# A macaron block of two SwiGLU layers around a pool and RWKV-7 mixer: the first modulation block summed on TensorE, the stored tiles multiplied from the first two rows of tiles on, and the modulation tiles of the first layer sent for three ahead

## The chip, the cores and the metric

The kernel runs on one core of a Trainium2 chip, in f32. A time is the device time of one execution in microseconds. Before the change three runs took 2119.42, 2113.76 and 2109.96 us, a median of 2113.76. One more execution was profiled and took 2117.75 us.

The engines are called as the profile calls them: PE is TensorE's matmul, PEld its weight load, DVE is VectorE, ACT is ScalarE, SP is SyncE, which here only sends DMAs.

## What is computed

A residual stream x of 256 tokens by 2048 passes three sublayers: a SwiGLU layer, a mixer, and a second SwiGLU layer. Each is normalised, modulated and gated by nine vectors of 2048 that come from one product of a conditioning vector with a wide matrix.

```python
mod = (jax.nn.silu(c) @ w_ada[l] + b_ada[l]).reshape(B, N_SUBLAYERS, N_MOD, D_MODEL)
...
h = modulate(rms_norm(x, gain_pre), shift, scale)      # h * (1 + scale) + shift
y = rms_norm(fn(h), gain_post)
return x + weight * (1 + gate[:, None, :]) * y
...
def swiglu(h, w_gate, w_up, w_down):
    return (jax.nn.silu(h @ w_gate) * (h @ w_up)) @ w_down
```

Here w_ada is 2048 by 18432 (151 MB), w_gate and w_up are 2048 by 5632, and w_down is 5632 by 2048. Every weight is read once. Only the first layer's beginning is touched by the change.

## The kernel before

**Precision.** PE multiplies in a fast f32 form, so each operand is split: hi is the operand rounded to that form, lo what is left. For the weights ACT writes hi (line 185) and DVE writes lo = raw - hi (line 186). The normalised input hT has both halves too. One weight product of the reference becomes three on PE: hi with both halves of hT, lo with the first.

**Tiles.** The model dimension is 16 rows of tiles (k = 0 to 15), each 128 long. In the first stage of a SwiGLU layer 20 of the 44 column tiles of w_gate and w_up are taken, in 10 loads of four tiles each. The first two loads (four columns of gate and four of up) keep their sums in four PSUM banks over all 16 rows. The other eight loads belong to the stored tiles (FF_SPILL = 16): each has two free banks for a block of rows, and what the block gives is copied by ACT (line 669) into SBUF, or added to it by DVE (line 671) in later blocks. The method outer runs this: for each block of rows it first makes hT for the block, then goes through the 10 loads.

**Blocks.** FIRST_BLOCKS cuts the rows into (0, 2), (2, 2), (4, 4), (8, 4), (12, 4): start and count. With MERGE = 4 the stored tiles leave out the first block and take rows 0 to 3 at once in the second. So the first block has two loads with 24 weight products each, and PE has nothing else until the second block's hT is there.

**Modulation.** hT of a block needs the shift and the scale vector for the block's rows (vectors 0 and 1). Their columns of w_ada come in DMAs (line 247, tiles called ada, 4 buffers of 512 KB; a block of two rows has eight such tiles), each tile holds two of the 16 contraction rows for both vectors, and DVE multiplies each by its column of silu(c) and adds it to acc (lines 255 and 257). Then PE sums acc over the partitions by a product with a vector of ones (line 201, mm<-ones,acc), DVE adds the bias (line 326, mod) and makes the gain (line 413, gs), PE transposes and normalises x by a product with a diagonal scale (mm<-scale,x), and ACT writes hT from that (line 425), and a copy (line 429, work) from which DVE makes the second half of hT (line 430).

**What sets the order.** A scheduler puts the instructions of each engine in one order when the kernel is built; each engine then works its queue strictly in that order, and so does SP. Buffers are rings: four raw, four ada, four hi and lo, eight PSUM banks. In the first layer ada_step sends for a part of the modulation and sums it at once. It is called at loads 1, 3 and 7 of a block (TICKS), and ada_finish does what is missing at the block's begin. In the second layer the generator ada_run does the same, but sends for each tile three ahead of its sum.

## Time and profile before

| | |
|---|---|
| median of three runs | 2113.76 us (2109.96 to 2119.42) |
| profiled execution | 2117.75 us |
| its span, first to last instruction | 2115.5 us |
| PE busy in the span | 2046.3 us, 97% |
| DVE busy | 1592.4 us, 75% |
| ACT busy | 1010.6 us, 48% |
| HBM read | 499.87 MB |

The page gives one execution. A busy share is over the whole span, and a busy PE is not a PE at its peak, since its pace depends on the granted clock. The views used below are the page's slices (40 equal parts of the span, 52.9 us each), windows (busy time of each engine in given stretches, with the granted clock and the DMA share), the timeline (instructions in order of time, equal neighbours merged, with the idle time before them and what ended it), and the chain of waits. In a row of the timeline the first number is the start, the second the duration of the whole row, and "x8" the number of instructions. One f32 product of the modulation (ones, scale) shows as two instructions.

### The profile page before, as it was taken

The numbers are of one execution on the slowest core, as the hardware profiler recorded it, in microseconds if no ns is written. First come the engines' busy times: TensorE is split into PE (matmuls) and PEld (weight loads), VectorE is DVE, ScalarE is ACT, GpSimd is POOL, SyncE is SP. The second block draws the span as 40 slices with busy tenths as digits, with TensorE's granted clock in tenths as the row PEclk, the third lists the DMA queues.
The fourth block names the chain that finished last, engine by engine and source line by source line (L and its number), as shares of the span: only waits on it lengthen the run. The fifth ranks groups of instructions, "written<-read, shape, count | busy, mean of one in ns | idle before, by whom it ended". The sixth has DMA issues, their size and how long they took to land.

```text
span 2115.5 us, 38899 instructions
## 1 busy us (share of the span) xinstructions
PE 2046.3 (97%) x16083; PEld 1825.0 (86%) x16083; DVE 1592.4 (75%) x2204; ACT 1010.6 (48%) x1483; POOL 0.2 (0%) x4
## 2 busy tenths in 40 slices
PE   3999999999999999999999999799999999999998
PEld 3999998888888887999999878699998888888887
DVE  6788897888887867688888885758699655555556
ACT  3544543444444455655555645353354344443453
POOL 0000000000000000000000000000000000000000
PEclk9999999999999999999999999899999999999999
DMA  8989888989899845565554564789587755655553
GB/s 301 359 309 320 288 287 319 324 314 320 312 328 325 278 144 188 175 193 152 158 163 140 161 235 140 247 303 321 179 313 283 244 195 183 192 186 198 184 196 120
DMA packets 315759, 506.62 MB, mean 239 GB/s; under 512 B 13013, under 2 KB 173886, under 8 KB 315070
## 3 DMA queue, kind: packets, MB, share of 16 engines
q1 hardware_dynamic: 314092, 500.78, 70.1%
q10 hardware_dynamic: 1490, 3.36, 0.5%
q8 instruction: 126, 2.06, 0.4%
q14 instruction: 51, 0.42, 0.1%
HBM read 499.87 MB, written 4.22 MB: 238 GB/s over the span
## 4 chain that ended last, share of the span: by engine, by line
PE 86%; DVE 2%; ACT 2%; DMA 1%; issue 0%; SPq 0%; DVEq 0%; ACTq 0%
PE mm L201 49%; PE mm L212 17%; PE mm L213 9%; PE sa L201 2%; PE ga L201 2%; PE zb L201 2%; PE pb L201 2%; PE sb L201 2%; PE y L201 1%; DVE lo L186 1%; ACT hi L185 1%; DMA raw<-in_w_in_dram 0%; DMA ada<-in_w_ada_dram 0%; DMA raw<-in_ffn_w_gate_dram 0%; DVE x L590 0%
## 5 line engine op out<-in xcount | busy, mean ns | idle before, releaser
L185 ACT CAST hi<-raw 128x1024 fp32r<-128x1024 f32 (+2 forms) x762 | 692.4, 914 | 871.2 <-PE mm L201 511.1
L186 DVE TENSOR_TENSOR lo<-raw,hi 128x1024 fp32r<-128x1024 f32 (+2 forms) x762 | 796.5, 1052 | 396.8 <-ACT hi L185 389.4
L201 PE MATMUL mm<-hT,hi 128*128 128x256 f32 x3648 | 669.4, 286 | 18.4 <-ACT hi L185 13.5
L201 PEld LDWEIGHTS mm<-hT,hi 128*128 128x128 f32 x3648 | 565.0, 190 | 33.9 <-ACT hi L185 14.3
L212 PE MATMUL mm<-hT,hi 128*128 128x512 f32 x1536 | 539.1, 394 | 0.0
L201 PE MATMUL mm<-hT,lo 128*128 128x256 f32 x1824 | 511.3, 281 | 1.3 <-DVE lo L186 1.3
L213 PE MATMUL mm<-hT,lo 128*128 128x256 f32 x1536 | 431.3, 281 | 0.0
L201 PE MATMUL mm<-hi,act 128*128 128x512 f32 (+1 forms) x1312 | 398.6, 384 | 0.0
L201 PEld LDWEIGHTS mm<-hT,lo 128*128 128x128 f32 x1824 | 345.7, 190 | 2.2 <-DVE lo L186 2.2
L212 PEld LDWEIGHTS mm<-hT,hi 128*128 128x128 f32 x1536 | 288.8, 188 | 67.6
L257 DVE SCALAR_TENSOR_TENSOR acc<-ada,csilu,acc 128x1024 f32<-128x1024 f32 (+1 forms) x247 | 300.2, 1215 | 45.1 <-DMA ada<-in_w_ada_dram 42.9
L213 PEld LDWEIGHTS mm<-hT,lo 128*128 128x128 f32 x1536 | 287.9, 187 | 0.2
L201 PEld LDWEIGHTS mm<-hi,act 128*128 128x128 f32 x1312 | 244.4, 188 | 48.7
L201 PE MATMUL mm<-lo,act 128*128 128x512 f32 (+1 forms) x656 | 252.0, 384 | 0.0
L201 PEld LDWEIGHTS mm<-lo,act 128*128 128x128 f32 x656 | 123.3, 188 | 24.4 <-DVE lo L186 0.3
L671 DVE TENSOR_TENSOR act<-act,mm 128x512 f32<-128x512 f32 x96 | 64.4, 680 | 2.1 <-PE mm L201 1.6
L257 DVE SCALAR_TENSOR_TENSOR ada<-x,csilu,ada 128x512 f32<-128x512 f32 (+1 forms) x45 | 41.3, 917 | 0.1
L201 PE MATMUL mm<-hi,work 128*128 128x512 f32 x128 | 40.7, 389 | 0.0
L425 ACT ACTIVATE hT<-mm,mod,gs 128x256 fp32r<-128x256 f32 x48 | 27.1, 570 | 17.7 <-PE mm L201 17.7
L201 PE MATMUL mm<-ones,acc 128*128 128x1 f32 x96 | 12.9, 263 | 20.7 <-DVE acc L257 20.7
L669 ACT COPY act<-mm 128x512 f32<-128x512 f32 x32 | 18.8, 587 | 28.8 <-PE mm L201 28.8
L201 PEld LDWEIGHTS mm<-ones,acc 128*128 128x128 f32 x96 | 12.9, 214 | 21.2 <-DVE acc L257 21.2
(402 smaller groups left out, 1686.6 us busy)
## 6 DMA issues: line engine op xcount, KB each, us to landing
raw<-in_ffn_w_down_dram SPq DMA_DIRECT2D x88, 1024.0 KB
raw<-in_ffn_w_gate_dram SPq DMA_DIRECT2D x86, 1024.0 KB
raw<-in_ffn_w_up_dram SPq DMA_DIRECT2D x86, 1024.0 KB
ada<-in_w_ada_dram SPq DMA_DIRECT2D x152, 512.0 KB
ada<-in_w_ada_dram SPq DMA_DIRECT2D x192, 256.0 KB
raw<-in_w_in_dram SPq DMA_DIRECT2D x34, 1024.0 KB
x<-in_w_ada_dram SPq DMA_DIRECT2D x64, 256.0 KB
raw<-in_w_out_dram SPq DMA_DIRECT2D x16, 1024.0 KB
```

The source lines that it names most:

```text
L185: a = nc.scalar.copy(hi, raw)
L186: d = nc.vector.tensor_tensor(lo, raw, hi.bitcast(F32), ALU.subtract)
L201: return self.pe(self.nc.tensor.matmul(ps, a, b, start=start, stop=stop))
L212: nc.tensor.matmul(ps.rearrange("p a t -> p (a t)"), hi, x.rearrange("p a t -> p (a t)"), start=start, stop=False)
L213: nc.tensor.matmul(ps[:, 0, :], lo, x[:, 0, :], start=False, stop=stop)
L257: self.later(nc.vector.scalar_tensor_tensor(acc, raw[:, i], ck, acc, ALU.mult, ALU.add))
L425: a = nc.scalar.activation(self.hT[:, k, 0, :], ps[:, j, :], AF.Identity, scale=g, bias=sh)
L669: nc.scalar.copy(part, bank)
L671: nc.vector.tensor_tensor(part, part, bank, ALU.add)
```

## The change

Three things change in the first layer; the second layer keeps its blocks under the new names LAST_BLOCKS and MERGES2.

1. The first modulation block is no longer summed by DVE. ada_first gives each 128 by 128 piece of the 16 contraction rows to PE as weights, with the column of silu(c) as the moving operand, and PSUM adds up: 64 products into four columns of one bank. The ones product falls away.
2. FIRST_BLOCKS becomes (0, 2), (2, 2), (4, 2), (6, 2), (8, 4), (12, 4). MERGES1 says at which block's end the stored tiles are multiplied, and from which row: after rows 0 and 1, after rows 2 and 3, then rows 4 to 7 at once, and so on. So the first block has ten loads, and a stored tile gets one copy and four additions instead of one copy and three.
3. The further modulation blocks go through ada_run with a lag of three, paced by RATES: 1.2 tiles to a load in the first two blocks, 2 for the two loads of the third, 1.8 and 1.6 in the next two, none in the last.

```diff
-MERGE = 4
-FIRST_BLOCKS = ((0, 2), (2, 2), (4, 4), (8, 4), (12, 4))
-TICKS = (1, 3, 7)
+FIRST_BLOCKS = ((0, 2), (2, 2), (4, 2), (6, 2), (8, 4), (12, 4))
+LAST_BLOCKS = ((0, 2), (2, 2), (4, 4), (8, 4), (12, 4))
+MERGES1 = {2: 0, 4: 2, 8: 4, 12: 8, 16: 12}
+MERGES2 = {4: 0, 8: 4, 12: 8, 16: 12}
+RATES = (1.2, 1.2, 2, 1.8, 1.6, 0)
...
+    def ada_first(self, bank, between):
+        cols, _ = self.ada_tasks[0]
+        per, n = 512 // cols[0][2], cols[0][2] // P
+        last = (KD - 1, 2 * n - 1)
+        for kk in range(0, KD, per):
+            between(kk // per)
+            raw = self.ada_load(cols, kk, per)
+            for k in range(kk, kk + per):
+                for i in range(2 * n):
+                    self.mul(bank[:, i:i + 1], raw[:, k - kk, i // n, i % n * P:(i % n + 1) * P],
+                             self.csilu[:, k:k + 1], (k, i) == (0, 0), (k, i) == last)
+        self.ada_bias(cols, bank)
+        self.ada_pos = 4
...
     def outer(self, blocks, loads, block, tick, piece, merges=None):
...
-                if parts is not None and b0 + bn <= MERGE:
-                    if b0 + bn < MERGE:
+                if parts is not None:
+                    if b0 + bn not in merges:
                         tick(q, i)
                         continue
-                    k0, kn = 0, MERGE
+                    k0 = merges[b0 + bn]
+                    kn = b0 + bn - k0
...
     def begin(self, mm):
...
-        for i in range(5):
-            if i == 3:
-                for tt in range(2):
-                    self.load_x(tt)
-            if i == 1:
+        def between(n):
+            if n in (4, 5):
+                self.load_x(n - 4)
+            if n == 2:
...
-            if i < 4:
-                self.ada_step(mm)
+        self.ada_first(self.tile(mm, [P, 512], tag="mm"), between)
...
+            ada = self.ada_run(((1, 0), len(FIRST_BLOCKS) - 1),
+                               lambda n: self.tile(self.raws, [P, 4 * T], tag="ada", bufs=self.ada_bufs), 3, bank)
             def block(k0, n):
                 q = [b[0] for b in FIRST_BLOCKS].index(k0)
-                self.ada_finish(((1, 0), q), mm)
+                while self.ada_pos < self.ada_end[(1, 0), q]:
+                    next(ada)
                 self.pre_block(0, k0, n, mm)
             def tick(q, i):
-                if q == len(FIRST_BLOCKS) - 1:
-                    if i == 0:
-                        self.begin_rest(mm)
-                elif i in TICKS:
-                    self.ada_step(mm)
+                if q == len(FIRST_BLOCKS) - 1 and i == 0:
+                    for _ in ada:
+                        pass
+                    self.begin_rest(mm)
+                if q != 2 or i < 2:
+                    for _ in range(int((i + 1) * RATES[q]) - int(i * RATES[q])):
+                        next(ada, None)
```

What this does to the queues is shown at three places. A row names line, operation, output and inputs, with a number on each tile; "x4" stands for four products in a row.

On PE, at the begin of the program, before: acc_106 is DVE's sum for rows 0 and 1.

```order
L144 MATMUL mm_122<-consts_69,work_117 128x112
L144 MATMUL mm_128<-consts_69,work_126 128x128
L201 MATMUL mm_164<-ones_71,acc_106 128x1 x4
L201 MATMUL mm_211<-scale_182,x_92 128x128 x4
L201 MATMUL mm_196<-hT_94,hi_224 128x256
L201 MATMUL mm_197<-hT_94,hi_224 128x256
```

On PE, the same place now, from the third modulation tile (ada_144) on; the transposes of line 146 bring vectors into columns.

```order
L203 MATMUL mm_106<-csilu_95,ada_144 128x1 x8
L146 MATMUL mm_134<-consts_69,work_129 128x112
L146 MATMUL mm_140<-consts_69,work_138 128x128
L203 MATMUL mm_106<-csilu_95,ada_155 128x1 x8
L203 MATMUL mm_106<-csilu_95,ada_167 128x1 x8
L203 MATMUL mm_254<-scale_225,x_92 128x128
L203 MATMUL mm_106<-csilu_95,ada_179 128x1 x8
L203 MATMUL mm_106<-csilu_95,ada_190 128x1 x8
L203 MATMUL mm_254<-scale_225,x_92 128x128 x3
L203 MATMUL mm_106<-csilu_95,ada_201 128x1 x8
L203 MATMUL mm_239<-hT_94,hi_270 128x256 x2
```

The four ones products have given way to eight products for each of eight tiles, and the four scale products stand among them instead of behind the sum.

On ACT, at the end of the normalisation of x, before: scale_182 is the diagonal, hi_224 and hi_265 are the casts of the first two weight loads.

```order
L406 ACTIVATE scale_182<-consts_69,row_189 128x128
L185 CAST hi_224<-raw_222 128x1024
L185 CAST hi_265<-raw_252 128x1024
L425 ACTIVATE hT_94<-mm_211,mod_105,gs_208 128x256
L429 ACTIVATE work_210<-mm_211,mod_105,gs_208 128x256
L425 ACTIVATE hT_94<-mm_211,mod_105,gs_208 128x256
L429 ACTIVATE work_210<-mm_211,mod_105,gs_208 128x256
L185 CAST hi_346<-raw_344 128x1024
```

And now:

```order
L428 ACTIVATE scale_225<-consts_69,row_232 128x128
L447 ACTIVATE hT_94<-mm_254,mod_105,gs_251 128x256
L451 ACTIVATE work_253<-mm_254,mod_105,gs_251 128x256
L447 ACTIVATE hT_94<-mm_254,mod_105,gs_251 128x256
L451 ACTIVATE work_253<-mm_254,mod_105,gs_251 128x256
L187 CAST hi_270<-raw_265 128x1024
L187 CAST hi_303<-raw_298 128x1024
```

The first casts have moved from ahead of the hT activations to behind them.

On DVE, before: the end of the sum for rows 2 and 3 (acc_254), its bias, and the first differences of the block that it opens (lo_347, lo_394).

```order
L257 SCALAR_TENSOR_TENSOR acc_254<-ada_298,csilu_95,acc_254 128x512 x2
L257 SCALAR_TENSOR_TENSOR acc_254<-ada_303,csilu_95,acc_254 128x512 x2
L257 SCALAR_TENSOR_TENSOR acc_254<-ada_308,csilu_95,acc_254 128x512 x2
L257 SCALAR_TENSOR_TENSOR acc_254<-ada_313,csilu_95,acc_254 128x512 x2
L257 SCALAR_TENSOR_TENSOR acc_254<-ada_318,csilu_95,acc_254 128x512 x2
L326 TENSOR_TENSOR mod_105<-mm_323,cols_29_130 128x2 x2
L413 SCALAR_TENSOR_TENSOR gs_330<-mod_105,cols_25_124 128x2
```

On DVE, now: the end of the sum for rows 6 and 7 (acc_1016); lo_1192 and lo_1230 belong to the two kept loads of those rows, lo_1270 and lo_1298 to the first stored load of rows 4 to 7.

```order
L188 TENSOR_TENSOR lo_1192<-raw_1184,hi_1191 128x1024
L274 SCALAR_TENSOR_TENSOR acc_1016<-ada_1019,csilu_95,acc_1016 128x512
L188 TENSOR_TENSOR lo_1230<-raw_1219,hi_1229 128x1024
L274 SCALAR_TENSOR_TENSOR acc_1016<-ada_1024,csilu_95,acc_1016 128x512
L188 TENSOR_TENSOR lo_1270<-raw_1257,hi_1269 128x1024
L274 SCALAR_TENSOR_TENSOR acc_1016<-ada_1024,csilu_95,acc_1016 128x512
L188 TENSOR_TENSOR lo_1298<-raw_1257,hi_1297 128x1024
L274 SCALAR_TENSOR_TENSOR acc_1016<-ada_1077,csilu_95,acc_1016 128x512 x2
L274 SCALAR_TENSOR_TENSOR acc_1016<-ada_1082,csilu_95,acc_1016 128x512 x2
L274 SCALAR_TENSOR_TENSOR acc_1016<-ada_1117,csilu_95,acc_1016 128x512 x2
L348 TENSOR_TENSOR mod_105<-mm_1163,cols_29_142 128x2 x2
```

A sum that stood on DVE by itself is now spread over the two blocks of weight work ahead of it: its products alternate with the differences of the loads, and only the last six stand alone. Between the bias for rows 2 and 3 and the end of this sum DVE has 16 differences lo of 128x1024, 16 additions into stored tiles, 30 products and 2 starts of 512 columns, 4 differences for hT, 2 biases (two instructions each) and 2 gains.

More of the change, by code (lines that the diff above doesn't have):

```diff
@@ L227, in ada_begin @@
             else:
-                for q, (k0, n) in enumerate(FIRST_BLOCKS):
+                for q, (k0, n) in enumerate(FIRST_BLOCKS if vs == (1, 0) else LAST_BLOCKS):
                     tasks.append([(v, k0 * P, n * P) for v in vs])
@@ L323, in ada_mod, with ada_bias @@
                 self.mul(ps[32 * q:32 * q + 32, :], self.quads, sums[:, :, q])
+        self.ada_bias(cols, ps)
+    def ada_bias(self, cols, ps):
+        nc = self.nc
+        n = cols[0][2] // P
         for j, (v, c, _) in enumerate(cols):
@@ L632, in rows_block, with outer @@
                 done(*part, banks[b][:, :part[2]])
-    def outer(self, blocks, loads, block, tick, piece):
+    def outer(self, blocks, loads, block, tick, piece, merges=None):
         nc = self.nc
@@ L671, in outer, with ffn @@
                             nc.vector.tensor_tensor(part, part, bank, ALU.add)
-    def ffn(self, wg, wu, wd, every, ada, mm, actp, blocks, block, outer_tick, first, spill, spare, groups, post_begin, post_done, ahead):
+    def ffn(self, wg, wu, wd, every, ada, mm, actp, blocks, merges, block, outer_tick, first, spill, spare, groups, post_begin, post_done, ahead):
         nc = self.nc
@@ L724, in ffn @@
                 loads.append((w, (first + 2 * i) * P, 2 * P * len(parts), bank, parts))
-        self.outer(blocks, loads, block, outer_tick, 1024)
+        self.outer(blocks, loads, block, outer_tick, 1024, merges)
         for i, (gate, up) in enumerate(zip(*pss)):
@@ L1440, in block @@
             def block(k0, n):
-                while self.ada_pos < self.ada_end[(7, 6), [b[0] for b in FIRST_BLOCKS].index(k0)]:
+                while self.ada_pos < self.ada_end[(7, 6), [b[0] for b in LAST_BLOCKS].index(k0)]:
                     next(ada)
@@ L1449, in run @@
             self.ffn(I["ffn2_w_gate"], I["ffn2_w_up"], I["ffn2_w_down"], ADA_FFN2, lambda: next(ada, None), mm, actp,
-                     FIRST_BLOCKS, block, tick, FF_OUTER, FF_SPILL, (FF_SPILL + FF_OUTER) // 2 - 8, GROUPS,
+                     LAST_BLOCKS, MERGES2, block, tick, FF_OUTER, FF_SPILL, (FF_SPILL + FF_OUTER) // 2 - 8, GROUPS,
                      lambda *a: (list(ada), self.post_begin(2, 0.5, False, mm, *a)),
```

4 lines of the change are left out of this document (3 added, 1 removed).

## Prediction

> **What bounds the kernel now.** I read the page first, then the windows of the first 60 us, then the timeline of that stretch.
>
> ```profile
> span 2115.5 us, 38899 instructions
> ...
> PE 2046.3 (97%) x16083; PEld 1825.0 (86%) x16083; DVE 1592.4 (75%) x2204; ACT 1010.6 (48%) x1483; POOL 0.2 (0%) x4
> ...
> PE   3999999999999999999999999799999999999998
> ...
> PEclk9999999999999999999999999899999999999999
> ```
>
> TensorE (PE) is busy for 97% of the span, and its row of 40 slices is full nearly everywhere except the first slice, which holds 52.9 us. Work moved between the other engines counts only where it shortens or lengthens a PE wait, and nearly all that waiting is in the first 50 us. The windows cut it up:
>
> ```profile
> 20.00:30.00 10.00, 3.78 (x16) 3.48 (x16) 5.71 (x15) 5.82 (x12) 0.00 (x0) 1.00 1.07 357
> 30.00:40.00 10.00, 8.52 (x49) 8.31 (x48) 9.26 (x14) 1.93 (x4) 0.00 (x0) 1.00 0.55 166
> 40.00:50.00 10.00, 4.11 (x17) 3.81 (x18) 6.57 (x11) 3.03 (x5) 0.00 (x0) 0.66 1.01 357
> 50.00:60.00 10.00, 9.45 (x63) 9.04 (x63) 7.55 (x8) 4.00 (x7) 0.00 (x0) 0.83 1.05 384
> ```
>
> PE works 3.78 of the third ten microseconds, 8.52 of the next, 4.11 of the next, and from 50 us on it is full. So there are two holes: the start, and one around 40 us.
>
> ```profile
> 5.30 0.49 DVE L255 TENSOR_SCALAR acc<-ada,csilu 128x512 f32<-128x512 f32 x1 [1.91 <-DMA ada<-in_w_ada_dram]
> ...
> 22.37 0.75 DVE L257 SCALAR_TENSOR_TENSOR acc<-ada,csilu,acc 128x512 f32<-128x512 f32 x1 [1.01 <-DMA ada<-in_w_ada_dram]
> ...
> 25.42 0.75 DVE L257 SCALAR_TENSOR_TENSOR acc<-ada,csilu,acc 128x512 f32<-128x512 f32 x1
> ...
> 25.85 1.97 ACT L185 CAST hi<-raw 128x1024 fp32r<-128x1024 f32 x2
> ...
> 26.22 1.86 PE L201 MATMUL mm<-ones,acc 128*128 128x1 f32 x8 [14.65 <-DVE acc L257]
> ...
> 27.95 2.06 PE L201 MATMUL mm<-scale,x 128*128 128x128 f32 x8
> 28.12 0.23 DVE L326 TENSOR_TENSOR mod<-mm,cols 128x2 f32<-128x2 f32 x2 [1.96 <-PE mm L201]
> ...
> 30.04 0.56 ACT L425 ACTIVATE hT<-mm,mod,gs 128x256 fp32r<-128x256 f32 x1 [2.22 <-PE mm L201]
> ...
> 30.66 1.50 PE L201 MATMUL mm<-hT,hi 128*128 128x256 f32 x5 [0.66 <-ACT hT L425]
> ...
> 31.40 0.57 ACT L429 ACTIVATE work<-mm,mod,gs 128x256 f32<-128x256 f32 x1
> ```
>
> The first hole: VectorE (DVE) multiplies the first modulation tiles from 5.30 us, waits at 22.37 for a DMA, does its last product at 25.42, and then eight PE instructions sum over partitions (ones), eight normalise x (scale), DVE adds the bias, and ScalarE (ACT) writes hT. The first weight product starts at 30.66. The ACT casts of the first two weight pieces (hi, 25.85) were over by then.
>
> ```profile
> 34.94 0.41 PE L201 MATMUL mm<-hT,hi 128*128 128x256 f32 x1
> 35.15 0.41 PE L201 MATMUL mm<-hT,lo 128*128 128x256 f32 x1
> ...
> 36.42 0.40 PE L201 MATMUL mm<-hT,lo 128*128 128x256 f32 x2
> ```
>
> These first products come 0.21 us apart; the two from 36.42 on take 0.40 together, 0.28 of it the last one's own length, so 0.12. From 30.66 to about 36.2 PE runs at half its pace and loses some 2.7 us, though the granted clock of that window reads 1.00.
>
> ```profile
> 32.35 8.62 DVE L257 SCALAR_TENSOR_TENSOR acc<-ada,csilu,acc 128x512 f32<-128x512 f32 x11
> ...
> 38.89 0.28 PE L201 MATMUL mm<-hT,lo 128*128 128x256 f32 x1
> ...
> 42.07 3.11 DVE L257 SCALAR_TENSOR_TENSOR acc<-ada,csilu,acc 128x512 f32<-128x512 f32 x4 [1.10 <-DMA ada<-in_w_ada_dram]
> ...
> 45.24 1.87 PE L201 MATMUL mm<-ones,acc 128*128 128x1 f32 x8 [6.07 <-DVE acc L257]
> ...
> 46.97 2.06 PE L201 MATMUL mm<-scale,x 128*128 128x128 f32 x8
> ...
> 49.68 1.50 PE L201 MATMUL mm<-hT,hi 128*128 128x256 f32 x5 [0.66 <-ACT hT L425]
> ```
>
> The second hole: the two loads of rows 0 and 1 are used up at 38.89, and the sum for rows 2 and 3 is still on DVE (eleven products from 32.35, the last four from 42.07). PE resumes with ones at 45.24, and weight products at 49.68, 10.8 us later, again slowly:
>
> ```profile
> 44.00:45.00 1.00, 0.00 (x0) 0.00 (x0) 0.96 (x2) 0.00 (x0) 0.00 (x0) 0.50 1.02 379
> ...
> 54.00:55.00 1.00, 1.00 (x11) 1.00 (x10) 0.96 (x2) 0.00 (x0) 0.00 (x0) 1.00 1.02 373
> ```
>
> The granted clock is 0.50 at 44 us and 1.00 again at 54.
>
> ```profile
> 104.73 1.84 PE L201 MATMUL mm<-ones,acc 128*128 128x1 f32 x16
> 106.44 2.03 PE L201 MATMUL mm<-scale,x 128*128 128x128 f32 x16
> 108.23 0.62 PE L201 MATMUL mm<-hT,hi 128*128 128x256 f32 x3
> ```
>
> At full clock sixteen ones instructions take 1.71 us (104.73 to 106.44: 0.107 each) and sixteen scale ones 1.79. At 26.22 and 45.24 eight ones take 1.73: 0.21 or 0.22 each. A ones product and a product of the new first sum have the same form: 128x128 f32 weights, one moving column, two instructions each.
>
> **The change, part by part.** *First sum on PE.* It removes 16 DVE operations and 8 ones instructions and adds 64 products, that is 128 instructions. None of them waits for DVE, and DMA landed the first tile by 5.30. Are they at 0.21 or at 0.107? From 26.22 to 29.99 PE had 3.8 us of ones and scale instructions almost without a gap, and the weight products after it were still at 0.21. I take 0.21: 128 x 0.21 = 26.9 us from 5.3 on. The eight scale instructions now stand among them (2.1 us). The sum ends at 5.3 + 26.9 + 2.1 = 34.3; the two small transposes in between are put at nothing. On SP's queue the two halves of x now go out behind the fourth and the fifth tile, and from the fifth on a tile waits until PE has released the one four before it; at 16 x 0.21 = 3.4 us a tile the eighth goes out at about 19, and PE comes to it at 31. So PE, not a landing, sets the end.
>
> *The cast behind hT.* In the new ACT order the four activations of hT stand ahead of the first cast, not behind it. Bias and gain take 0.3 us, the four activations 1.9 (30.04 to 31.40 + 0.57), the cast 1.0 (half of 1.97). First weight product at 34.3 + 0.3 + 1.9 + 1.0 = 37.5, against 30.66.
>
> *Ten loads instead of two on rows 0 and 1.* This fills the hole at 39 us: 240 weight products stand there now where 48 stood. Their pace:
>
> ```profile
> 171.20 58.67 PE mm L201 x497
> ```
>
> 58.67 us / 497 = 0.118 us. Ramp 2.7, then 220 products at 0.118 (26.0) until the ones of rows 2 and 3 stand in the PE order (0.9): their bias is at 37.5 + 29.6 = 67.1. The sixteen copies of stored tiles (ACT) lie beside it; DVE has 10 differences and 16 products in it, which end sooner.
>
> *The sums two blocks ahead.* From that bias to the end of the sum for rows 6 and 7, the new DVE order holds 16 differences (lo), 16 additions into stored tiles, 30 products and 2 starts of 512 columns.
>
> ```profile
> 148.80 1.28 DVE L671 TENSOR_TENSOR act<-act,mm 128x512 f32<-128x512 f32 x2
> 150.08 1.23 DVE L186 TENSOR_TENSOR lo<-raw,hi 128x1024 fp32r<-128x1024 f32 x1
> 151.22 2.60 DVE L257 SCALAR_TENSOR_TENSOR acc<-ada,csilu,acc 128x1024 f32<-128x1024 f32 x2
> ```
>
> ```profile
> L257 DVE SCALAR_TENSOR_TENSOR acc<-ada,csilu,acc 128x512 f32<-128x512 f32 x16 | 12.0, 751 | 1.6 <-DMA ada<-in_w_ada_dram 1.1
> ```
>
> Start to start in this busy stretch: two additions 1.28, a difference 1.14. A product of 512 columns takes 0.751. So DVE needs 16 x 1.14 + 16 x 0.64 + 32 x 0.75 = 18.2 + 10.2 + 24.0 = 52.4 us (the four small differences of hT left out). In that time PE has 20 + 240 + 48 = 308 products, 36.3 us, and some 2.5 us of ones and scale: 38.8. It then waits 13.6 us. Queued behind the waiting ones on PE are the scale products and all further weight products, those of the stored tiles on rows 4 and 5 too, since these are merged with rows 6 and 7. The restart costs what it cost at 45.24: 4.4 us from ones to weight products, and 1.9 for the half pace from 49.68 to about 53.4. So PE is at full pace on rows 6 and 7 at an effective 67.1 + 52.4 + 4.4 + 1.9 = 125.8.
>
> *The sum.* By then 528 weight products are done. In the profiled run they are done at 108.23 + 48 x 0.118 = 113.9. Difference **+11.9 us**. Afterwards both kernels do the other 1,392 of the stage's 1,920 products (20 column tiles, two matrices, 16 rows, 3 each) with PE bound: for rows 6 and 7 DVE has 13 differences, 14 additions and 16 products of 1,024 columns (14.8 + 9.0 + 16 x 1.30 = 44.6 us, 1.30 being half the last row of the DVE fence), against 432 x 0.118 = 51 us on PE. So DVE does not hold it further, and it has no gap to give back either: what the start loses stays lost, since PE is full to the end. The sixteen extra additions into stored tiles, and the sums of half the width that come with the narrower blocks, are in the 52.4 us. Other stages keep their code.
>
> Costs without a row of their own: the pace of the new products is between 0.107 and 0.208 us (13 us apart; I take the upper, as above). DVE's handoffs inside the 52.4 us lie between nothing and the 4.4 us of one restart; I take nothing.
>
> The profiled execution took 2117.75 us; the median of the runs is 2113.76. Added to the run it is 2129.6, to the median, 4 us lower, 2125.7, which is the forecast.
>
> The Trainium skill, TensorE: Matmul & The Clock Gate, Part 1, says that PE starts at half clock and goes to full after one busy window of about 3.4 us. By it the new sum would run at full clock from about 9 us and the whole come out near no change. The trace agrees for dense weight products (slow for 5.5 us, then full) and disagrees for the 3.8 us of ones and scale at 26.22, after which the pace was still half.
>
> **Rivals.** *A, the sum brings PE to full pace.* For it: PE is filled without a gap far longer than the 3.8 us at 26.22, and sixteen ones plus sixteen scale at 104.73 did not lower the clock. Against: those 3.8 us. The last tile lands one tile of 0.52 MB after the one waited for at 22.37, at 357 GB/s by 23.9; its sixteen instructions end at 25.6; first weight product 28.8; no ramp; bias of rows 2 and 3 at 55.7; + 52.4 + 4.4 + 1.9 = 114.4. That is +0.5 us: 2114.
>
> *B, faster: DVE keeps up.* If DVE's queue between that bias and the third sum were 14 us shorter (below 38.8), PE would not stop at rows 6 and 7 and would be there at 67.1 + 38.8 + 2.5 (the block's own ones, scale, bias and hT) = 108.4: -5.5 us, 2108; with A, 28.8 + 26.9 + 38.8 + 2.5 = 97.0: -17, 2097. For it: DVE idles ahead of the bias, and could take products of the second sum there if the order let it. Against: in the new order they stand behind the bias, and the steps are read from a stretch where DVE was full.
>
> *C, slower still: tiles land late.* From 37 us to the third sum's end 20 modulation tiles and 20 loads of 0.52 MB and two of 1.05 must come: 23 MB, 64 us at 357 GB/s, and 82 are there. If DMA averages 250 GB/s as in its poorer windows (166 at 30 to 40), that is 92, and 10 us are added: 2136. For it: SP sends in order, so a load that waits for its slot holds back the tile behind it.
>
> **How the numbers follow.** Forecast 0.57, A 0.24, B 0.10 (half of it together with A), C 0.09. About 0.5% (10.6 us) is what a measurement of this kernel can tell from no change. The forecast lies 1.3 us above that bound and its parts may err by 6, so two thirds of its chance are slower, the rest no change; with C slower has 0.47. B with A gives 0.05 to faster, and the low tail of A 0.02. The range runs to 2137, past C, and down to 2104, which takes in A and B alone and leaves out B with A.
>
> **What would show it.** Right: ones-like products 0.21 apart until about 34 us; first weight product near 37.5; a PE hole of 12 to 18 us shortly before 120 us that ends with ones after a DVE product; clock 0.50 there. Wrong at the first step: products 0.107 apart by 15 us. Wrong at the last: no hole above 5 us after the start, or one that ends on a DMA.

## The result, and the profile after

| | before | after |
|---|---|---|
| median of the runs | 2113.78 us (2109.96 to 2119.42, 4 runs) | 2138.85 us (2135.39 to 2142.48, 4 runs) |
| ratio, 95% interval | | 1.0111 (1.0087 to 1.0135) |
| profiled execution | 2117.75 us | 2136.1 us |
| its span | 2115.5 us | 2134.3 us |

The change makes the kernel slower: 25 us at the medians, 18.4 us between the two profiled executions. The forecast was 11.9 us more, with a range that ended at 2137. The sign was right, the size was not, and the measured median lies above that range.

The page of the kernel after, its first lines and two rows of its 40 slices:

```profile
span 2134.3 us, 39193 instructions
...
PE 2069.0 (97%) x16203; PEld 1845.2 (86%) x16203; DVE 1586.9 (74%) x2223; ACT 1007.7 (47%) x1483; POOL 0.2 (0%) x4
...
PE   8989999999999999999999999799999999999998
...
PEclk9989999999999999999999999899999999999999
```

PE is busy for 22.7 us more than before, and that is no sign of health: the first sum keeps it busy from the begin. The first slice reads 8 where it read 3, and the third shows the clock down. The windows of the kernel after (start and end, then busy time of PE, PEld, DVE, ACT, POOL, the granted clock, the DMA share, GB/s):

```profile
20.00:30.00 10.00, 10.00 (x48) 10.00 (x48) 0.64 (x3) 1.26 (x5) 0.00 (x0) 1.00 0.87 274
30.00:40.00 10.00, 6.56 (x31) 6.18 (x30) 4.35 (x9) 5.64 (x8) 0.00 (x0) 1.00 0.65 202
40.00:50.00 10.00, 10.00 (x77) 10.00 (x77) 6.79 (x9) 2.01 (x4) 0.00 (x0) 1.00 0.96 326
67.93:124.26 56.33, 41.88 (x332) 39.50 (x331) 51.84 (x74) 20.92 (x26) 0.00 (x0) 0.94 0.89 290
110.00:120.00 10.00, 5.24 (x44) 5.03 (x43) 10.00 (x13) 2.10 (x2) 0.00 (x0) 0.88 1.05 360
120.00:130.00 10.00, 5.58 (x24) 5.31 (x25) 5.87 (x12) 1.80 (x4) 0.00 (x0) 0.50 0.94 321
158.00:190.00 32.00, 27.71 (x229) 26.50 (x228) 25.50 (x31) 12.58 (x17) 0.00 (x0) 1.00 0.83 295
```

The old hole at 40 us is gone (10.00). A new one lies at 115 to 125, with DVE at 10.00 before it and the clock at 0.50 behind it, and PE waits again for 4.3 us between 158 and 190. The timeline of PE in the kernel after (start, duration of the row, count, idle time before it and what ended it):

```profile
4.43 10.37 PE L203 MATMUL mm<-csilu,ada 128*128 128x1 f32 x48 [1.29 <-DMA ada<-in_w_ada_dram]
...
22.35 6.83 PE L203 MATMUL mm<-csilu,ada 128*128 128x1 f32 x32
...
30.46 3.41 PE L203 MATMUL mm<-csilu,ada 128*128 128x1 f32 x16
37.27 1.22 PE L203 MATMUL mm<-hT,hi 128*128 128x256 f32 x4 [3.40 <-ACT hi L187]
...
124.41 1.83 PE L203 MATMUL mm<-ones,acc 128*128 128x1 f32 x8 [9.17 <-DVE acc L274]
126.10 2.06 PE L203 MATMUL mm<-scale,x 128*128 128x128 f32 x8
127.81 0.78 PE L203 MATMUL mm<-hT,hi 128*128 128x256 f32 x2
```

The sum's instructions come 0.213 us apart to the very end (6.83 / 32, 3.41 / 16), the first weight product waits for the cast behind hT, and the hole ends with ones that waited 9.17 us for DVE's sum. The weight products of rows 6 and 7 follow 3.4 us behind these ones.

### The profile page after: what moved, and what is told of

The parts are those of the page before. It is cut to its first block, busy times and chain, and to the rows that moved or that the text cites. A ratio compares the mean times of both kernels' runs of the same rounds, so it can differ in the third digit from the quotient of the medians.

```text
span 2134.3 us, 39193 instructions
## 1 busy us (share of the span) xinstructions
PE 2069.0 (97%) x16203; PEld 1845.2 (86%) x16203; DVE 1586.9 (74%) x2223; ACT 1007.7 (47%) x1483; POOL 0.2 (0%) x4
## 4 chain that ended last, share of the span: by engine, by line
PE 83%; DMA 8%; DVE 5%; ACT 2%; issue 2%; SPq 1%; DVEq 0%; ACTq 0%
PE mm L203 47%; PE mm L214 16%; PE mm L215 8%; DMA ada<-in_w_ada_dram 4%; DVE lo L188 2%; PE ga L203 2%; PE sa L203 2%; PE zb L203 2%; PE sb L203 2%; PE pb L203 2%; DMA raw<-in_ffn_w_gate_dram 1%; DVE acc L274 1%; PE y L203 1%; DMA raw<-in_ffn_w_up_dram 1%; ACT hi L187 1%
## 5 line engine op out<-in xcount | busy, mean ns | idle before, releaser
L203 PE MATMUL mm<-hT,hi 128*128 128x256 f32 x3648 | 663.6, 285 | 25.1 <-ACT hi L187 18.2
L274 DVE SCALAR_TENSOR_TENSOR acc<-ada,csilu,acc 128x1024 f32<-128x1024 f32 (+1 forms) x247 | 292.4, 1184 | 91.5 <-DMA ada<-in_w_ada_dram 89.8
L695 DVE TENSOR_TENSOR act<-act,mm 128x512 f32<-128x512 f32 x112 | 74.7, 681 | 2.4 <-PE mm L203 2.3
L730 ACT ACTIVATE silu<-silu 128x512 f32<-128x512 f32 x24 | 15.2, 633 | 62.0 <-DVE silu L729 62.0
L733 ACT CAST act<-silu 128x512 fp32r<-128x512 f32 x24 | 14.9, 619 | 39.9 <-DVE silu L731 39.9
L693 ACT COPY act<-mm 128x512 f32<-128x512 f32 x32 | 18.8, 586 | 25.1 <-PE mm L203 24.8
```

The source lines that it names most:

```text
L203: return self.pe(self.nc.tensor.matmul(ps, a, b, start=start, stop=stop))
L274: self.later(nc.vector.scalar_tensor_tensor(acc, raw[:, i], ck, acc, ALU.mult, ALU.add))
L693: nc.scalar.copy(part, bank)
L695: nc.vector.tensor_tensor(part, part, bank, ALU.add)
L730: last = nc.scalar.activation(s, s, AF.Silu)
L733: nc.scalar.copy(a[:, :, 0, :], s)
```

## The experiments

One row of the timeline serves as a milestone for the first stage: DVE's bias for rows 12 to 15 (mod of 4 columns, the last of the blocks), with 1,440 weight products done ahead of it in each kernel. Before the change it stands at 228.89 us. Two later experiments, e13 and e18, leave this stage as it was before the change and have it at 228.09 and 227.00, and two executions of the changed kernel differ by 2.4, so a step under 3 us says nothing.

| kernel | bias of rows 12 to 15, us | time against the kernel before, 95% interval |
|---|---|---|
| changed | 248.22 | 1.0111 (1.0087 to 1.0135) |
| e0, changed again | 245.78 | 1.0098 (1.0079 to 1.0117) |
| e1, DVE sums the first block | 239.95 | 1.0064 (1.0050 to 1.0078) |
| e4, wide block (4, 4) | 240.75 | 1.0064 (1.0043 to 1.0085) |
| e5, both | 232.36 | 1.0049 (1.0037 to 1.0062) |
| e2, before with the first sum on PE | 235.41 | 1.0048 (1.0032 to 1.0063) |

### e0, the changed kernel again

> The changed kernel itself, beside the others on one chip. Its runs so far fell into two pairs, 2135.4 and 2136.1, and 2141.6 and 2142.5, and its profiled execution shows 18.8 us more span than the kernel before, its median 25 us more. If the profile has the whole loss, the median lies 18 to 20 us above the kernel before on this chip (ratio 1.0085 to 1.0095); if there is a loss that the profiled execution did not have, 23 to 27 us (1.011 to 1.013).

2136.61 us against 2115.25, 1.0098 (1.0079 to 1.0117), with a profiled span of 2133.9. The interval takes in both answers, 16.7 to 24.7 us. The loss is about 21 us here and 25 there. The two profiled executions show 18.4 and 18.8 us of it, by their spans against 2115.5.

### e1, the first sum back on DVE

```diff
-        self.ada_first(self.tile(mm, [P, 512], tag="mm"), between)
+        for i in range(4):
+            between(2 * i)
+            between(2 * i + 1)
+            self.ada_step(mm)
```

> The changed kernel, but the first modulation block is summed by DVE again, as before the change; the ten loads on rows 0 and 1, the narrow blocks and the tiles sent for three ahead stay. Theory S (each loss has its own place: 6.6 us by the first sum at 0.213 us an instruction, about 6.7 by DVE's queue up to the sum for rows 6 and 7, about 6 in rows 8 to 11 by the order of the DMAs on SP): the first weight product stands 5 to 7 us earlier than the 37.3 us of the changed kernel, the later holes move with it and keep their size, and the time is 5 to 7 us below the changed kernel, about +18 against the kernel before at the medians. Rival R (the late holes are set by transfers or by DVE's total from the program's begin, so that an earlier start only waits longer later): first weight product as early, but the time within 2 us of the changed kernel, +23 to +27 against the kernel before.

The bias of rows 12 to 15 in e1:

```profile
239.95 0.23 DVE L348 TENSOR_TENSOR mod<-mm,cols 128x4 f32<-128x4 f32 x2 [0.99 <-PE mm L203]
```

It comes 5.8 to 8.3 us earlier than in the changed kernel; the time is 13.7 us above the kernel before, by the ratios 7 to 10 below the changed one (e0 and the first result), a little more than S had. The early start is kept through the holes of the first stage. Rival R, by which it would be lost again, falls.

### e2, the first sum on PE and nothing else

> The kernel before, with the first modulation block summed by PE and nothing else of the change. Theory S: the first weight product moves from 30.7 to about 37.5 us, and since on DVE the products of the second sum stand behind the first differences lo, DVE's freedom before 37 us is not used; the second hole ends at about 51 us in place of 45, and the time is 5 to 7 us above the kernel before. Rival R: the second sum's tiles land while PE still sums the first block, DVE takes them at once, the second hole vanishes and the time is within 2 us of the kernel before.

```profile
235.41 0.23 DVE L346 TENSOR_TENSOR mod<-mm,cols 128x4 f32<-128x4 f32 x2 [0.99 <-PE mm L201]
```

The milestone is 6.5 us later than before, as S had it; the time is 1.0048 (1.0032 to 1.0063), 11 us at the medians and 4 to 6 more than S. In the profile 3.5 of them come between 757 and 888 us, at the begin of the mixer, whose code is the same. The second hole did not vanish: the ones of rows 2 and 3 still wait for DVE, 7.29 us here and 6.07 before the change:

```profile
52.25 1.87 PE L201 MATMUL mm<-ones,acc 128*128 128x1 f32 x8 [7.29 <-DVE acc L272]
```

### e3, sixteen additions less

```diff
                         if k0 == 0:
                             nc.scalar.copy(part, bank)
-                        else:
+                        elif k0 > 2:
                             nc.vector.tensor_tensor(part, part, bank, ALU.add)
```

> The changed kernel without the sixteen additions into the stored tiles on rows 2 and 3 (what the stored tiles get from rows 2 and 3 is left out of the result); their weight products stay. It takes 16 x 0.64 = 10.2 us off DVE's queue between the bias of rows 2 and 3 (67.9 us) and the end of the sum for rows 6 and 7 (124.3 us). Theory S (DVE's queue sets the hole): the ones products of rows 6 and 7 start 8 to 11 us earlier, near 115 us, and the time falls by 8 to 11 us against the changed kernel. Rival T (that sum waits for its tiles, by the order of the DMAs on SP): the sum ends within 3 us of 124 us, DVE shows idle time ahead of the products instead, and the time falls by less than 3 us.

This kernel leaves out what rows 2 and 3 give to the stored tiles, so it serves only to time the queue.

The ones of rows 6 and 7 in the timeline of e3:

```profile
115.53 1.42 PE L203 MATMUL mm<-ones,acc 128*128 128x1 f32 x8 [3.14 <-DVE acc L274]
```

They stand 8.9 us earlier than 124.41, where 10.2 us of additions were taken away, and the wait is 3.14 us in place of 9.17. DVE's queue sets this hole, not the landing of tiles. The time is 1.0075 (1.0059 to 1.0090), 5 to 8 us under the changed kernel by the ratios (S: 8 to 11). Part of the gain is given back: at the milestone e3 is 11.2 us behind the kernel before, and at a PE instruction behind the blocks (mm<-sums, 408.21 us before the change, 422.37 in e3) 14.2, of which more below.

### e4 and e5, the narrow blocks undone

```diff
-FIRST_BLOCKS = ((0, 2), (2, 2), (4, 2), (6, 2), (8, 4), (12, 4))
+FIRST_BLOCKS = ((0, 2), (2, 2), (4, 4), (8, 4), (12, 4))
-RATES = (1.2, 1.2, 2, 1.8, 1.6, 0)
+RATES = (1.2, 1.8, 1.8, 1.6, 0)
```

with "q != 2 or i < 2" dropped; e5 has e1's edit too.

> The changed kernel with the first block summed by DVE again and with the wide block (4, 4) in place of (4, 2) and (6, 2), so that only the ten loads on rows 0 and 1 and the tiles sent for three ahead are left of the change (paces 1.2, 1.8, 1.8 and 1.6 tiles to a load). On SP modulation tiles and weight loads now alternate up to row 12, with never more than two tiles in a row between loads. Theory S: bias of rows 2 and 3 near 60 us; DVE then has 10 differences (11.4), 16 additions (10.2) and 16 products of 1,024 columns (20.8), 42.4 us, so the sum for rows 4 to 7 ends near 103, weight products are at full pace at an effective 109 with 480 done (the kernel before: 108.2), and rows 8 to 11 lose nothing, since SP's order is mended: within 3 us of the kernel before, about 24 below the changed one. Rival U (the loss in rows 8 to 11 is DVE's or PE's and has nothing to do with SP's order): the same up to row 7, and then 5 to 7 us more, so that it is 5 to 10 us above the kernel before.

> The changed kernel with the wide block (4, 4) in place of (4, 2) and (6, 2), paces as in e5; the first sum stays on PE. Against e1, e5 had 7.6 us less at the bias of rows 12 to 15 (232.4 against 240.0 us). Theory S (the parts of the loss add up, since each is a stretch of its own in which PE has nothing): the same step here, 245.8 to 248.2 us becomes 237 to 242, and the time falls by 6 to 9 us against the changed kernel. Rival Y (with the later start the wide block's longer sum, 16 products of 1,024 columns, ends no earlier than the two narrow ones): the bias stays within 3 us of the changed kernel's and so does the time.

The same milestone in e5, and then in e4:

```profile
232.36 0.23 DVE L348 TENSOR_TENSOR mod<-mm,cols 128x4 f32<-128x4 f32 x2 [0.99 <-PE mm L203]
```

```profile
240.75 0.23 DVE L348 TENSOR_TENSOR mod<-mm,cols 128x4 f32<-128x4 f32 x2 [0.99 <-PE mm L203]
```

The narrow blocks, with their paces, cost 7.6 us (e1 to e5) or 5.0 to 7.5 (changed kernel to e4), the first sum on PE 8.4 (e5 to e4) or 5.8 to 8.3 (changed kernel to e1). e4's time is 7 to 10 us below the changed kernel's by the ratios (S: 6 to 9). e5 is 3.5 us behind the kernel before at this milestone, where S had at most 3. Its time is 11 us behind, which is rival U's number, but not U's place: the further loss comes between 411 and 757 us, behind all blocks. In the first stage the parts add up: about 7, 7 and 3.5 make 17.5, against 16.9 and 19.3 measured.

### e6 and e7, wide products against the slow pace

```diff
+        wide = self.hT[:, KD - 1].rearrange("p a t -> p (a t)").bitcast(F32)
+        nc.vector.memset(wide, 0.0)
+        self.wide = lambda n: [nc.tensor.matmul(idle, self.ident, wide, start=True, stop=True) for idle in
+                               [self.tile(mm, [P, 512], tag="mm")] * n]
+        self.wide(4)
         self.ada_first(self.tile(mm, [P, 512], tag="mm"), between)
```

and in e7 one `self.wide(1)` behind each tile of the sum.

> The changed kernel with four idle products of 512 columns (zeros, into a bank that nobody reads) ahead of the first sum, some 7 us of PE work at the half pace. Theory P (the sum's products are slow only because nothing before them raised PE's pace, and they hold a pace once it is raised): behind the idle products the sum's instructions come 0.107 us apart to the end, the sum ends near 27 us, the first weight product stands near 30 without a ramp behind it, and the time is 8 to 10 us below the changed kernel. Theory Q (products of one column do not count as load): the pace goes back to 0.213 within 3 to 7 us, the sum ends at 33 to 37 us, and the time is within 3 us of the changed kernel.

The begin of PE's timeline in e6, then three windows:

```profile
3.16 6.21 PE L1405 MATMUL mm<-hT,consts 128*128 128x512 f32 x8
9.21 8.00 PE L203 MATMUL mm<-csilu,ada 128*128 128x1 f32 x48
...
17.50 6.83 PE L203 MATMUL mm<-csilu,ada 128*128 128x1 f32 x32
```

```profile
5.00:10.00 5.00, 5.00 (x15) 2.52 (x14) 0.00 (x0) 0.06 (x1) 0.00 (x0) 1.00 1.04 345
10.00:15.00 5.00, 5.00 (x33) 5.00 (x32) 0.00 (x0) 1.03 (x1) 0.00 (x0) 0.67 0.86 298
15.00:20.00 5.00, 5.00 (x26) 5.00 (x25) 1.05 (x5) 2.06 (x6) 0.00 (x0) 0.50 0.88 288
```

Behind the wide products 48 instructions take 8.00 us where they took 10.37: some 20 of them at 0.107, the rest at 0.213. PE is 5.00 of 5.00 busy in all three windows, and the granted clock goes from 1.00 to 0.67 to 0.50. Theory Q: products of one column do not hold the clock. The bias behind the sum stands at 36.31 (33.91 in the changed kernel), and the time, 1.0117 (1.0095 to 1.0138), is the changed kernel's.

> The changed kernel with idle wide products (512 columns of zeros, into banks that nobody reads): four ahead of the first sum, as in e6, and one behind each of its eight tiles. In e6 the sum's instructions came 0.107 us apart for one stretch behind the idle products and then 0.213 again. Theory Q (the pace follows wide products, and products of one column let it fall): with one wide product for every sixteen instructions the pace holds 0.107; PE then has 9.4 us up to the first tile's end of waiting, 128 x 0.107 = 13.7, 8 x 0.78 = 6.2 and the scale products 0.9, so the sum ends near 30, the first weight product stands near 33.5 and has no ramp: the bias of rows 2 and 3 near 61 in place of 67.9, the time 5 to 7 us below the changed kernel. Rival X (the clock goes by the clock's own schedule or by the whole chip, not by what the core's products are): the pace falls back to 0.213 by about 15 us as in e6, the sum ends later than 40, and the time is 5 us or more above the changed kernel.

In e7 the scheduler put single wide products (two instructions, as at 10.62) behind some of the tiles, and four of them together at 19.57:

```profile
8.91 1.84 PE L203 MATMUL mm<-csilu,ada 128*128 128x1 f32 x16
10.62 1.10 PE L1406 MATMUL mm<-hT,consts 128*128 128x512 f32 x2
...
17.06 2.65 PE L203 MATMUL mm<-csilu,ada 128*128 128x1 f32 x16
19.57 6.23 PE L1406 MATMUL mm<-hT,consts 128*128 128x512 f32 x8
25.64 1.84 PE L203 MATMUL mm<-csilu,ada 128*128 128x1 f32 x16
...
33.84 3.41 PE L203 MATMUL mm<-csilu,ada 128*128 128x1 f32 x16
```

With one wide product between tiles the sum keeps 0.107 for 9 us (16 in 1.84); from 17 us it slows, full again behind the four wide ones (25.64), and at half pace at the end, where none stands between (33.84). The wide products cost more than the pace gave: 1.0130 (1.0117 to 1.0144), 4 to 7 us above the changed kernel by the ratios, where Q had 5 to 7 below and rival X 5 or more above. Against X's reason speaks the full pace up to 17 us. What these rows show is that the pace follows wide products; how many it takes is open.

### e11 and e20, where the late loads come from

e11 chains the DMAs of loads and modulation tiles on SP in the order of the program:

```diff
+    def sp(self, op):
+        if self.sp_ordered:
+            if self.sp_last is not None:
+                self.after(op, self.sp_last, "order")
+            self.sp_last = op
```

> The changed kernel with SP's DMAs of the first stage held to the order in which the program writes them: one or two modulation tiles behind each weight load, in place of up to thirteen tiles in a row ahead of the load of rows 8 to 11. Nothing else is changed. Theory S (the waits of 158 to 190 us on hi, and on lo behind it, come from loads that SP sends late): these waits vanish, the bias of rows 12 to 15 comes 2 to 5 us earlier than 248.2 us, and the time falls by as much. Rival V (the waits come from DVE's queue, which is behind since the hole): the same waits on lo stay, and the time is within 1.5 us of the changed kernel.

The waits of PE in e11 from 25 to 260 us (who waited for whom, us in all, times, longest):

```profile
PE mm L210 <- ACT hi L194: 13.8, 6, 4.7
PE mm L210 <- DVE lo L195: 4.1, 5, 1.8
```

The bias of rows 6 and 7 came 4.4 to 5.2 us earlier (121.07), and the waits of 158 to 190 us went, but waits on hi took their place from 100 to 140 us, and at the milestone (245.61) nothing is left that e0's 245.78 does not have. The time, 1.0095 (1.0069 to 1.0121), tells neither theory from the other. The order on SP alone does not mend it.

e20 has six buffers for modulation tiles in place of four (`self.phase(ctx, 4, 4, 6)`).

> The changed kernel with six buffers for modulation tiles in place of four. Up to the sum for rows 6 and 7 the order of the DMAs on SP stays but for a few tiles that go out earlier. In the changed kernel, between 67.9 and 124.3 us DVE works 51.8 us and idles 4.5, 2.2 of it for a cast whose load SP had sent late, and SP itself waits 62 us in 67 to 190 us for DVE to give a tile's buffer back, with the weight loads queued behind. Theory S (DVE's work sets the hole, its idle 4.5 us come from SP standing at a tile without a buffer): SP's waits for DVE shrink by half or more, DVE's idle time in that stretch falls by 2 to 4 us, the bias of rows 6 and 7 comes at 121 to 124 us in place of 125.5 to 126.3, and that of rows 12 to 15 at 240 to 244 in place of 245.8 to 248.2; the hole itself stays over 5 us, since DVE's 51.8 us of work stay. Rival T (the loads are late because the transfers are full): no bias earlier by more than 1.5 us.

SP's largest entry in its waits between 67 and 190 us, in the changed kernel and then in e20, and e20's window that answers to the last one shown above:

```profile
SPq L264 <- DVE acc L274: 49.8, 26, 7.7
```

```profile
SPq L264 <- DVE acc L274: 26.6, 19, 4.1
```

```profile
158.00:190.00 32.00, 31.53 (x267) 31.12 (x267) 27.01 (x35) 14.22 (x18) 0.00 (x0) 1.00 0.92 328
```

With the entry of acc L272, SP's 62.4 us of waits for these sums become 37.8, where S had half or less. The waits of 158 to 190 us are gone (PE 31.53 of 32, after 27.71 and, in e0, 28.57), so those came from SP standing at a tile without a buffer with weight loads behind it. But the bias of rows 6 and 7 stayed at 126.30, where S had 121 to 124. From its bias of rows 2 and 3 to the end of the sum for rows 6 and 7, e20's DVE idles for 3.6 us, against 4.5 in the changed kernel, where S had 2 to 4 less:

```profile
68.95:124.27 55.32, 40.68 (x332) 39.27 (x331) 51.75 (x74) 20.53 (x26) 0.00 (x0) 0.95 0.86 283
```

```profile
119.80 1.23 DVE L188 TENSOR_TENSOR lo<-raw,hi 128x1024 fp32r<-128x1024 f32 x1 [1.32 <-ACT hi L187]
```

Its waits for casts fall from 3.0 us to the 1.3 at 119.80, and its waits for PE's results rise from 1.1 to 1.9 us. So more buffers move DVE's waits and shorten them by less than a microsecond. The milestone is at 244.15, the time 1.0079 (1.0064 to 1.0094).

### e10, e12, e13, e17, e18 and e21, a smaller dose

If the hole is DVE's queue against PE's products, less of the change should do better. e10 is the kernel before with six loads on rows 0 and 1:

```diff
-MERGE = 4
-TICKS = (1, 3, 7)
+MERGE, EARLY = 4, 6
+TICKS = ((0, 1, 3, 5), (1, 3, 7), (1, 3, 7), (1, 3, 7))
...
-                if parts is not None and b0 + bn <= MERGE:
+                if parts is not None and b0 + bn <= MERGE and not (early and i < EARLY):
...
-                elif i in TICKS:
+                elif i in TICKS[q]:
```

> The kernel before, with one part of the change in a smaller dose: on rows 0 and 1 six loads in place of two (144 products in place of 48; four of the eight loads of the stored tiles are taken early and get one addition more), DVE sums the first block as before, blocks as before, and the four parts of the second sum begun at loads 0, 1, 3 and 5. Theory S (a hole is DVE's queue up to the next bias against the products that PE has until then): the second sum needs 16 x 0.75 and six differences at 1.14 from about 26 us, so it ends near 45; PE has 144 products from 30.7, that is 2.7 + 17, until about 50, and the hole at 39 to 50 us is filled. For the sum of rows 4 to 7 DVE then has 16 differences (18.2), 8 additions (5.1) and 16 products of 1,024 columns (20.8), 44 us, against 336 products on PE (39.6) and some 4 of the block's own: no new hole over 4 us. The time falls 5 to 10 us below the kernel before. Rival W (the hole only moves to rows 4 to 7, as it did in the change): within 3 us of the kernel before, with a wait for DVE's sum near 90 us.

The milestone is at 225.06, 3.8 us earlier than before; the time is 1.0015 (1.0002 to 1.0028), 3.5 us later at the medians, where S had 5 to 10 below. W's wait for DVE's sum near 90 us is not there. The lead is lost behind the blocks. Two rows of e10's timeline there, DVE's and PE's:

```profile
397.12 1.28 DVE L257 SCALAR_TENSOR_TENSOR acc<-ada,csilu,acc 128x1024 f32<-128x1024 f32 x1 [4.14 <-DMA ada<-in_w_ada_dram]
...
400.79 0.38 PE L213 MATMUL mm<-hT,lo 128*128 128x256 f32 x1 [1.69 <-DVE lo L186]
```

DVE stands 4.14 us at a modulation tile that has not landed; two differences lo are queued behind, and PE waits for one. This takes 2.0 of the 3.8 us (mm<-sums stands at 406.40, against 408.21 before); the rest goes between 440 and 760 us and was not traced to a cause.

e12 (e10 and tiles sent two ahead in that stage) and e13 (the same on the kernel before); step takes the place of ada_step in the call of ffn:

```diff
+            run = []
+
+            def step():
+                if not run:
+                    run.append(self.ada_run((3,), lambda n: self.tile(self.raws, [P, 4 * T], tag="ada", bufs=self.ada_bufs),
+                                            2, lambda: self.tile(mm, [P, 512], tag="mm")))
+                for _ in range(4):
+                    next(run[0], None)
...
-                     lambda *a: (self.ada_finish((3,), mm), self.post_begin(0, 0.5, True, mm, *a)), lambda tt: None, True)
+                     lambda *a: (list(run[0]), self.post_begin(0, 0.5, True, mm, *a)), lambda tt: None, True)
```

> e10, and in the stage behind the blocks (the other 24 column tiles of the first layer) the modulation tiles are sent for two ahead of their sums instead of being summed at once; pace and number of tiles stay. e10 was 3.8 us ahead of the kernel before at the bias of rows 12 to 15 and 0.7 behind at 411 us: at 397 us DVE waited 4.14 us for a modulation tile, and the difference lo queued behind it kept PE waiting. Theory Z (the lead is given back to such waits of DVE's queue on a tile sent too late): the wait of PE on lo between 380 and 420 us vanishes, the lead of 3 to 4 us is kept to the end, and the time is 2 to 6 us below the kernel before. Rival D (the lead is given back to the transfers as a whole, which are nearly full from 240 to 420 us): PE waits elsewhere in that stage, on hi for a load, and the time is within 2 us of the kernel before or above it.

> The kernel before with only the second part of e12: modulation tiles sent for two ahead of their sums in the stage behind the blocks. The kernel before has no PE wait between 240 and 400 us. Theory Z: nothing to win there, the time within 3 us of the kernel before; so a gain of e12 over this one is the two loads' own. Rival D: the tiles sent earlier take the place of weight loads on SP, and the time is 3 us or more above the kernel before.

Both were far slower, 1.0176 (1.0158 to 1.0194) and 1.0186 (1.0172 to 1.0200), for a reason that neither theory had, and against what the expectation says of the number of tiles: ended at vector 3, the generator left 24 tiles to the mixer. A window of e13 there, and the same window before the change:

```profile
1260.00:1320.00 60.00, 22.55 (x162) 18.28 (x161) 38.72 (x51) 5.62 (x10) 0.00 (x0) 0.63 0.76 262
```

```profile
1260.00:1320.00 60.00, 58.71 (x352) 47.65 (x349) 34.01 (x64) 28.80 (x59) 0.00 (x0) 0.94 0.49 176
```

e17 and e18 end the generator where the kernel before stood at the end of the layer (50 parts).

> e12 again, now with as many modulation tiles in the first layer as the kernel before has. e12 stopped at the end of the third vector and left 24 tiles to the mixer; there it lost 38 us between 907 and 1331 us, while up to 907 us it had kept its lead of 5 to 7 us over the kernel before. Theory Z (a lead from the first stage is kept where DVE's queue does not wait for tiles sent too late): the lead of 4 to 7 us stands at 411, 757 and 1331 us, and the time is 3 to 7 us below the kernel before (ratio 0.9967 to 0.9986). Rival D (the lead is given back to the transfers as a whole): PE waits on hi or lo between 380 and 760 us, and the time is at the kernel before's or above.

> e13 again, with as many modulation tiles in the first layer as the kernel before: the kernel before, with tiles sent for two ahead in the stage behind the blocks and nothing else. Theory Z: that stage of the kernel before has no PE wait, so nothing is to be had: within 3 us of the kernel before, and e17's gain over it is that of the two loads. Rival D: 3 us or more above.

e17 keeps its lead: no wait of PE between 380 and 420 us is left, and its span is 2110.3 against 2115.5. Its time, 0.9992 (0.9980 to 1.0004), is no different from that of the kernel before, nor from e18's, 0.9992 (0.9982 to 1.0002). So theory Z holds in the profile (its rival's waits are not there), and the 3 to 7 us that it promised do not show in the runs.

> e17 with six buffers for modulation tiles. e17's profile was 5.2 us below the kernel before, its median only 2.2, with an interval that takes in no change. Theory S: waits of SP on a tile's buffer delay loads in all of the first layer, so two more buffers give 1 to 4 us more: 3 to 8 us below the kernel before (ratio 0.9962 to 0.9986). Rival T: the loads are not late by buffers; within 2 us of e17, ratio 0.9980 to 1.0000.

e21, with six buffers, has the milestone at 223.98 and takes 2113.73 us against 2118.05, 0.9977 (0.9967 to 0.9987). It is 4 to 5 us faster than the kernel before and the only version here whose interval lies below 1. That is the number S had, but S's reason does not show: e21's interval overlaps e17's, and at the milestone it is 1.3 us behind e17 (223.98 and 222.71), so no gain by the buffers shows in the first stage. Six buffers on the kernel before alone were not run.

## Why the prediction was right, and where it failed

- **First sum at the slow pace**: right. 0.213 us an instruction to the end, first weight product at 37.27 where the text had 37.5. Undone (e1) or done alone (e2) it is worth 5.8 to 8.4 us in the first stage. Rival A, the sum that brings PE to full pace, is refuted by the changed kernel itself and by e6.
- **Ten loads on rows 0 and 1**: right. The bias of rows 2 and 3 stands here, where the text had 67.1:

```profile
67.93 0.23 DVE L348 TENSOR_TENSOR mod<-mm,cols 128x2 f32<-128x2 f32 x2 [1.17 <-PE mm L203]
...
96.28 1.23 DVE L188 TENSOR_TENSOR lo<-raw,hi 128x1024 fp32r<-128x1024 f32 x1 [2.17 <-ACT hi L187]
...
119.58 4.68 DVE L274 SCALAR_TENSOR_TENSOR acc<-ada,csilu,acc 128x512 f32<-128x512 f32 x6
```

- **DVE's queue up to the sum for rows 6 and 7**: the mechanism right, and its work too. In the window from 67.93 to 124.26, quoted above, DVE is busy for 51.84 us; the text had 52.4. The step that failed is the term beside it: "DVE's handoffs inside the 52.4 us lie between nothing and the 4.4 us of one restart; I take nothing". They took 56.33 - 51.84 = 4.5 us (3.8 in e0). By the timeline 3.0 of them are waits for ACT's casts, the largest the 2.17 us at 96.28, and 1.1 are waits for PE. The sum ended at 124.3, not 119.5. Two smaller terms went the other way: from the ones to the weight products it took 3.4 us and not 4.4, and the kernel before has its 528 products done at 115.0 and not at 113.9. Counted weight product by weight product in the traces, PE at full pace behind the hole is 14.7 us behind the kernel before (13.6 in e0), and not 11.9. e3 shows that the hole is DVE's.
- **The size of the hole**: the text put all of PE's waiting, 13.6 us, into one hole of 12 to 18 us. PE was idle for 56.33 - 41.88 = 14.5 us in that window, but only 9.17 of them in the hole; the other 5.3 are small waits ahead of it, for lo and for hT.
- **"DVE does not hold it further"**: failed by 4.6 us (3.3 in e0). Between 158 and 190 us PE waited on hi, lo and hT, because SP's queue stood at modulation tiles without a buffer: in e20, with six buffers, PE is 15.3 us behind the kernel before both after the hole and at the milestone. In the changed kernel the loss at the milestone is 19.3 us instead of 14.7. The text had weighed DVE's work against PE's there, and not SP's queue, which rival C named for another place.
- **"What the start loses stays lost"**: true of the changed kernel in the end, 19.3 us at the milestone and 18.8 at the last instruction, with up to 22.5 in the mixer between them. It is not a law: by PE's instructions e1, e3 and e10 lost 2 to 3 us more between the milestone and mm<-sums at 408 us. e10 and e17 show one way how, a tile that lands late in front of lo.
- **Blocks of two rows**: the text named their cost as a part of the 52.4 us and gave it no price of its own. With their paces it is 5 to 8 us (e4; e1 against e5), as much as the first sum.
- **The rest of the median**: the forecast loss was 11.9 us, the measured one 25.1. In the traces 2.8 us of this miss arose up to the hole's end and 4.6 more up to the milestone. The two profiled executions differ by 18.4 us. The other 6.7 lie in which executions were profiled: the one before was 4.0 us above its median, the one after 2.7 below. In e0, with more runs of the kernel before, the medians differ by 21 us, with an interval that takes in 18.4; whether anything beyond that is real stays open.

Rival B (DVE keeps up) fell with the hole. Rival C had the time nearly right, 2136, but its late loads account for about 5 us behind the hole and not for ten ahead of it, so this is in part luck.

## What to carry to other kernels

Add up the work on the queue that sets a hole, and then some idle time too: here DVE's queue, which waits for casts and for PE's results, idled for 4.5 us beside 51.8 of work, 9%. Work moved to an idle engine is free only if nothing that starts the kernel waits for it there. And when tiles are sent further ahead, look at the queue that sends them: here a tile without a free buffer held back the loads behind it.

## What the hardware showed

- In e6 PE's granted clock fell from 1.00 (5 to 10 us) to 0.50 (15 to 20 us) while PE was busy without a gap, with 128 by 128 weights and one moving column in each instruction; behind the four products of 512 columns the pace had been full, 0.107 us an instruction. The Trainium skill (TensorE: Matmul & The Clock Gate, Part 1) lets the clock fall after an idle window of about 3.4 us and rise after a busy one. By the rows here a stream of products of one column does not act as a busy window: some 29 us of little else (4.43 to 33.9 in the changed kernel) left the pace at 0.213 us.
- The granted clock reads 1.00 from the program's begin, also where the pace is half: 0.213 us an instruction between 20 and 30 us in the kernel after, with 1.00 in that window. In these traces the column is not to be trusted before the first change of the clock; the pace is.
- Two executions of one program in the same stage, with the same order of instructions, differed by 2.4 us at the milestone (248.22 and 245.78).
